# Gates' operands from GpSimd, the first pair's in u's weight buffers, and two groups of loads moved, in a decoder block

## The chip, the cores and the metric

One core of a Trainium2 chip runs the whole program. The metric is the device time of one execution in microseconds (us); the kernel before takes 2845.56 us (median of three runs, 2842.94 to 2846.51).

## What is computed

The reference is one decoder block on a sequence of 2048 tokens of width 1024. Cut to what matters here:

```python
h    = _rmsnorm(x, norm_pre_mix)
proj = h @ w_in                      # 1024 -> 5376 columns: q, k, v, u, z, gate_a, gate_b
u, z = gelu(proj[U0:Z0]), gelu(proj[Z0:GA0])
gate_a, gate_b = sigmoid(proj[GA0:GB0]), sigmoid(proj[GB0:])
y_attn = dilated_attention(q, k, v)  # 3 groups of 4 heads, merged by their log-denominators
y_gmlp = u * (spatial(layernorm(z)) + b_spatial)
merged = gate_a * (y_attn @ w_branch_attn) + gate_b * (y_gmlp @ w_branch_gmlp)
x = x + _rmsnorm(merged @ w_out)
a = relu(_rmsnorm(x) @ w_mlp_in)
x = x + _rmsnorm((a * a) @ w_mlp_out)
```

## The kernel before

Every product in float32 is made of three matmuls: each operand is split into a rounded part `hi` and a rest `lo`, and `mm3` (L91) adds hi·hi, hi·lo and lo·hi in PSUM. `split` (L68) makes both: `hi` by a copy on ACT, DVE or POOL, `lo` by a subtraction on DVE or POOL.

**Order of work.** TensorE's (PE's) instructions stay in the order in which the program is written; for ACT, DVE, POOL and the DMA queue of SP a scheduler of the framework fixes an order when the kernel is built. Each engine then works through its own list strictly in order, and an instruction that waits holds up all behind it. The stages up to the merge of the branches are:

1. q, k and v for all tokens (to L379), stored in DRAM.
2. `plain_1` (L468): u and z for the second half of the tokens. z is normalized, goes through the spatial product in `sz_out` (L419), is multiplied by u and stored as `ygd`. Weights come through `load_w` (L239) into the pool `wp`: tag `w` with six buffers, tag `raw` with two.
3. `seven` (L509): the gates of all tokens, and u of the first half, by Strassen's seven products. A pair is 256 columns of `w_in`; there are 16 pairs for the gates and two for u. For each pair `prepare` (L515) loads 1 MB of weights into `wr`, makes four sums of its quarters on POOL (L531 to L535), and splits seven operands (A11, S2, A12, S3, S1, A22, S4) into four places of `A_room`, `hi` on ACT, `lo` on DVE. A product is 12 matmuls of 512 columns (L560). Operand m+4 is prepared when product m is done, so a place is filled three products ahead of its use.
4. Attention: 48 units (`attn_unit`, L661), written between the steps of `seven` (a step is three matmuls) by the loop at L832. PE makes scores (`s`), DVE adds the mask and takes the maximum, one instruction of 128x4 on DVE (`nm`, L709) turns the maxima into the bias of ACT's exponentials, PE transposes (`pT`), ACT and DVE copy and split the result (`ph`, `pf`), PE multiplies by v (`pv`), ACT copies (`pvs`), PE transposes (`po`), and DVE reduces into `o` (L758). Scores, `pT`, `pv` and `po` share four PSUM buffers.
5. The combination (`combine`, L762): for each of four blocks of 512 tokens the three groups' results `A` are loaded, weighted on DVE (L769 to L786), added up (L788, L789: on DVE for the first block, else on POOL), transposed on PE (`yt`, L794) and stored. It too is written between steps of `seven`, the last 52.
6. `plain_0`: z for the first half, with the weights `z_w` loaded at L858; then the merge, for which `w_branch` is split into `wb` at L879.

After that come the output projection and the MLP, which the change does not touch.

**What lies around the change.** The first pair can only be prepared once z's weights have left `wp` (L816), since the pool `ap` with `wr` takes their room, and once the last of `H` has left tag `B12`, which `A_room` takes over (L512). The lines that set the steps around it are

```python
    steps(2 * 4 * 8 + 2 * 32 - 72 + 1)
    ew1.close()
    ap = stack(e1, "ap", 1)
    sm = stack(e1, "sm1", 2)
    steps(9)
    sz_out(*late.pop(0))
```

and attention's first loads follow `sz_out`, whose buffers they take.

Of the kernel before, what the change touches and what calls it, by code (L numbers as in the profile page):

```python
# [8 lines left out]
F32 = mybir.dt.float32  # L9
# [7 lines left out]
P = 128  # L17
# [24 lines left out]
def block_kernel(ctx, tc, a, out):  # L42
# [24 lines left out]
    def split(hi, lo, src, hi_eng="act", lo_eng="dve"):  # L67

        if hi_eng == "act":
            act.activation(hi, src, AF.Copy)  # L70
        elif hi_eng == "pool":
            pool.tensor_scalar(hi, src, 1.0, 1.0, op0=OP.mult, op1=OP.mult)  # L72
        else:
            dve.tensor_copy(hi, src)
        if behind_product is not None and lo_eng == "dve":
            behind_product.append((lo, src, f32(hi)))
        else:
            (pool if lo_eng == "pool" else dve).tensor_sub(lo, src, f32(hi))  # L78
# [82 lines left out]

    e1 = ExitStack()
    hp = stack(e1, "hp", 1)
    ew1 = ExitStack()
    wp = stack(ew1, "wp", 2)
    sm = stack(ew1, "sm", 2)
    st = stack(ew1, "st", 2)


    H = {}  # L170
# [60 lines left out]
    def w_src(i, kk):  # L231
        return a["w_in"][i, :, kk * 4:(kk + 1) * 4, :]

    n_w = 6

    def load_w(i, name):

        ws = []
        for kk in range(2):  # L239
            w = wp.tile([P, 2, 4, 256], F32R, name=f"{name}_{kk}", tag="w", bufs=n_w)  # L240
            raw = wp.tile([P, 4, 256], F32, name=f"{name}_r{kk}", tag="raw", bufs=2)
            split_in(w, w_src(i, kk), raw)
            ws.append(w)
        return ws
# [20 lines left out]
    def run(steps):  # L265
        for _ in steps:
            pass
# [197 lines left out]
    def plain_1():  # L465

        for q, (wi, kind, n, half) in enumerate(queue):
            if kind == "z" and n == 1:  # L468
                continue
            want(q)  # L470
            want(q + 1)
            if kind == "z" or (kind, n) == ("u", 1):
                want(q + 2)
            w = loaded[q]
            if kind == "z":
                for ci in range(2):
                    yield from z_chunk(zps[half], (w, loaded[q + 1]), half * 2 + ci)
                continue
            for ci in range(2):
                c = half * 2 + ci  # L480
                for m in range(2):
                    p = psum_mm(f"{kind}_{n}{m}{c}")
                    yield from steps_T(w, m, c, p)
                    t = st.tile([P, 512], F32, name=f"{kind}t_{n}{m}{c}", tag="ev", bufs=3)
                    act.activation(t, p, AF.Gelu_apprx_tanh)
                    sp.dma_start(u_d[n * 2 + m, :, c * 512:(c + 1) * 512], t)

# [8 lines left out]
    def load_op(half, name):  # L496

        pl = hp if name[0] == "B" else tp
        w = pl.tile([P, 2, 4, 512], F32R, name=f"{name}_b{half}", tag=name)
        if name[0] == "T":  # L500
            src = t1_d[half, :, int(name[1]) - 1]
        else:
            k = 4 * (int(name[1]) - 1)
            src = h_d[2 * half + int(name[2]) - 1, :, k:k + 4]
        for k in (0, 2):
            split_in(w[:, :, k:k + 2], src[:, k:k + 2], None, "act")
        ops[half, name] = w

    def seven():  # L509

        seq = [(p, *t) for p in pairs for t in SEVEN]
        room = hp.tile([P, 2, 4, 512], F32R, name="A_room", tag="B12")  # L512
        left, raws = {}, {}

        def prepare(m):  # L515
            if m >= len(seq):
                return
            pair, i, name, _ = seq[m]
            wi = pair[0]
            if name == "A11":  # L520
                raws["t"] = ap.tile([P, 2560], F32, name=f"wr_{m}", tag="wr")
                sp.dma_start(raws["t"][:, :2048], a["w_in"][wi].rearrange("p k c -> p (k c)"))
            t = raws["t"]
            q = t[:, :2048].rearrange("p (k c) -> p k c", c=256)
            a11, a12, a21, a22 = (q[:, k:k + 4, f:f + P] for f in (0, P) for k in (0, 4))
            s1 = t[:, 2048:].rearrange("p (k c) -> p k c", c=P)
            w = room[:, :, m % 4].rearrange("p o (k c) -> p o k c", k=4)
            split(w[:, 0], w[:, 1], dict(A11=a11, S2=a11, A12=a12, S4=a12, S3=a21, S1=s1, A22=a22)[name])
            left[m] = w
            if name == "A11":  # L530
                pool.tensor_add(s1, a21, a22)  # L531
                pool.tensor_sub(a21, a11, a21)
                pool.tensor_sub(a11, s1, a11)  # L533
            elif name == "A12":
                pool.tensor_sub(a12, a12, a11)  # L535

        def put(pair, f, ci, t):
            _, dst, n, half = pair
            if dst is u_d:
                act.activation(t, t, AF.Gelu_apprx_tanh)  # L540
            c = 2 * half + ci
            sp.dma_start(dst[2 * n + f, :, c * 512:(c + 1) * 512], t)

        for m in range(4):
            prepare(m)
        for m, (pair, i, name, bn) in enumerate(seq):
            half = pair[3]
            if i in (1, 6, 5):
                p = psum_mm(f"s{i}_{m}")
                if i == 1:  # L550
                    pa = p
                elif i == 6:
                    pb = p
                else:
                    pc = p
            p = {1: pa, 2: pa}.get(i) or ({6: pb, 7: pb, 4: pb}.get(i) or pc)
            w, h = left.pop(m), ops[half, bn]
            for k in range(4):
                for n, (l, r) in enumerate(((0, 0), (0, 1), (1, 0))):
                    pe.matmul(p, w[:, l, k, :], h[:, r, k, :], start=i in (1, 6, 5) and not k and not n,  # L560
                              stop=k == 3 and n == 2, skip_group_check=True)
                yield
            if i == 1:
                xs = ap.tile([P, 512], F32, name=f"xs_{m}", tag="xs", bufs=2)
                act.activation(xs, p, AF.Copy)
            elif i == 2:
                c1 = ap.tile([P, 512], F32, name=f"c1_{m}", tag="u", bufs=3)
                act.activation(c1, p, AF.Copy)
                put(pair, 0, 0, c1)
            elif i in (6, 7):  # L570
                u = ap.tile([P, 512], F32, name=f"u{i}_{m}", tag="u", bufs=3)
                dve.tensor_add(u, xs, p)
                if i == 6:
                    u6 = u
                else:
                    u7 = u
            elif i == 5:
                dve.tensor_add(u7, u7, p)
                put(pair, 1, 1, u7)
            elif i == 4:  # L580
                dve.tensor_add(xs, xs, p)
                put(pair, 1, 0, xs)
            else:
                dve.tensor_add(u6, u6, p)
                put(pair, 0, 1, u6)
            if half and pair[2] == 7:
                load_op(0, bn)
            prepare(m + 4)

    def plain_0():  # L590
# [9 lines left out]
    def filler():  # L600
        yield from plain_1()
        yield
        yield from seven()
        ended.append(True)
        yield
        yield from plain_0()

    fill = filler()

    def steps(n):  # L610
        for _ in range(n):
            next(fill, None)
# [199 lines left out]
    next(sg)  # L812
    steps(72)
    next(sg)
    steps(2 * 4 * 8 + 2 * 32 - 72 + 1)
    ew1.close()  # L816
    ap = stack(e1, "ap", 1)
    sm = stack(e1, "sm1", 2)
    steps(9)
    sz_out(*late.pop(0))  # L820
    ez.close()
    at1 = stack(e1b, "at1", 2, side="right")
    mask = at1.tile([P, 256], F32, name="mask", bufs=1)
# [1 line left out]
    attn_open(0, 0)  # L825
    attn_load(0, 0, 0)
    attn_load(0, 0, 1)
    steps(8)
    at = stack(e1b, "at", 2, side="right")
    steps(12)  # L830
    for n in range(len(units) + 1):
        u = None  # L832
        if n < len(units):
# [20 lines left out]
    e1b.close()  # L854
    n_w = 4
    wp = stack(e1, "wp2", 2)
    st = stack(e1, "st2", 1)
    z_w = [load_w(11 + n, f"w_z{n}0") for n in range(2)]  # L858
    ec = ExitStack()
    cb = stack(ec, "cb", 2, side="right")  # L860
    cs = [combine(c) for c in (2, 3, 0, 1)]
# [1 line left out]
        next(cs[n])  # L863
        next(cs[n])
    for n in range(4):
        steps((24, 14, 9, 5)[n])
        next(cs[n])
        if n < 2:
            next(cs[n + 2])
            next(cs[n + 2])  # L870
    ec.close()
    while not ended:
        steps(1)
    etp.close()
# [11 lines left out]
    steps(32)  # L886
    next(sg)
    run(fill)
    e1.close()


# [937 lines left out]
```

## Time and profile before

| | |
|---|---|
| median of three runs | 2845.56 us (2842.94 to 2846.51) |
| the profiled execution | 2839.19 us, of which the span of instructions 2837.5 us |
| PE matmuls | busy 2697.8 us, 95% of the span, 13196 instructions |
| DVE | busy 1695.6 us, 60% |
| ACT | busy 1131.5 us, 40% |
| POOL | busy 1054.2 us, 37% |
| granted clock of PE, mean | 0.978 of full speed |

PE is the engine with the most work. So one reads where PE stands idle or runs at the lower of its two clock levels (1.2 instead of 2.4 GHz, 0.5 in the profile), who ended each of its waits, and what stood ahead of that instruction in its engine's list. Busy time of the other engines matters only where it sits in such a chain. The stages above lie at 0 to 437.6 us (1), to 531.8 (2), to 574.4 (the start of 3 alone), to 1068.2 (3 and 4), to 1146.3 (5), and to the end (6 and the rest).

### The profile page before, as it was taken

To read this page: it belongs to the slowest core of one execution; us is meant where nothing else is said; L and a number is where in the kernel's file an instruction comes from. 1 tells how busy PE (TensorE), PEld (TensorE's weight loads), DVE (VectorE), ACT (ScalarE), POOL (GpSimd) and SP (SyncE) were. 2 spreads that over 40 slices of the span, in tenths; PEclk is the share of its full clock that TensorE was granted. 3 is DMA by queue.
4 is the path that set the end of the run, shared out by engine and by line. 5 is a ranking of instruction groups with operands and counts; after the bars stand their busy time and mean duration, and the time that the engine had idled before them with its cause. 6 is when DMAs were issued, how large, how long until landed. Compare 5 with 4: busy or idle time off the path is not lost. (4 is left out here: it accounts for less than half of the span.)

```text
span 2837.5 us, 36367 instructions
## 1 busy us (share of the span) xinstructions
PE 2697.8 (95%) x13196; PEld 2254.6 (79%) x13196; DVE 1695.6 (60%) x2839; ACT 1131.5 (40%) x2283; POOL 1054.2 (37%) x845
## 2 busy tenths in 40 slices
PE   8999999889989996899999899999999999999998
PEld 8889888778867885877778688888887877777787
DVE  5665563355566557565556654555445777777766
ACT  4213112145555443244344554555544222333334
POOL 2442541221111123311403532223323566776745
PEclk9999999999989998999999999999999999999999
DMA  8747654276575646465646734554334222222236
GB/s 282 231 141 226 213 151 146 92 234 185 178 259 181 179 156 225 124 227 158 197 146 219 234 115 123 159 192 131 100 118 135 66 82 82 85 86 82 82 98 214
DMA packets 327284, 449.17 MB, mean 158 GB/s; under 512 B 19008, under 2 KB 201536, under 8 KB 324800
## 3 DMA queue, kind: packets, MB, share of 16 engines
q1 hardware_dynamic: 239408, 395.71, 44.1%
q10 hardware_dynamic: 87696, 51.13, 6.0%
q8 instruction: 104, 1.70, 0.2%
q14 instruction: 76, 0.62, 0.1%
HBM read 295.58 MB, written 151.19 MB: 157 GB/s over the span
## 5 line engine op out<-in xcount | busy, mean ns | idle before, releaser
L1680 PE MATMUL ya<-T_spots,s 128*128 128x512 f32 x1272 | 313.3, 392 | 4.7 <-DVE acc L1688 2.7
L1680 PEld LDWEIGHTS ya<-T_spots,s 128*128 128x128 f32 x1272 | 239.0, 188 | 59.1 <-issue 4.5
L70 ACT ACTIVATE s<-sraw 128x768 fp32r<-128x768 f32 (+1 forms) x184 | 126.0, 695 | 358.5 <-POOL sraw L1479 199.4
L560 PE MATMUL s<-T_b,A_room 128*128 128x512 f32 x864 | 228.7, 406 | 1.3 <-DVE A_room L78 0.7
L1140 PE MATMUL aa<-B,A 128*128 128x512 f32 x768 | 186.6, 395 | 8.1 <-ACT xs L1154 5.8
L1111 POOL TENSOR_TENSOR s<-w1r 128x512 f32<-128x512 f32 x32 | 43.1, 1348 | 395.8 <-DVE S L78 330.3
L560 PEld LDWEIGHTS s<-T_b,A_room 128*128 128x128 f32 x864 | 160.4, 193 | 33.4 <-DVE A_room L78 1.4
L78 DVE TENSOR_TENSOR s<-sraw,s 128x512 fp32r<-128x512 f32 x171 | 163.7, 980 | 34.8 <-ACT s L70 33.2
L1140 PEld LDWEIGHTS aa<-B,A 128*128 128x128 f32 x768 | 145.1, 190 | 42.2 <-ACT xs L1154 6.2
L78 DVE TENSOR_TENSOR A_room<-wr,A_room 128x512 fp32r<-128x512 f32 x126 | 101.4, 808 | 117.8 <-ACT A_room L70 113.7
L1680 PE MATMUL yc<-T_spots,s 128*128 128x512 f32 x624 | 164.3, 394 | 3.6 <-POOL T_spots L78 3.6
L531 POOL TENSOR_TENSOR wr<-wr 128x512 f32<-128x512 f32 x18 | 24.4, 1353 | 360.6 <-DMA wr<-in_w_in_dram 352.3
L97 PE MATMUL x<-B,wq 128*128 128x512 f32 x384 | 150.7, 392 | 2.7 <-DVE wq L78 2.7
L95 PE MATMUL x<-B,wq 128*128 128x512 f32 x384 | 150.7, 393 | 0.7 <-POOL wq L72 0.7
L96 PE MATMUL x<-B,wq 128*128 128x512 f32 x384 | 150.4, 392 | 0.0
L1680 PEld LDWEIGHTS yc<-T_spots,s 128*128 128x128 f32 x624 | 115.9, 188 | 33.7 <-POOL T_spots L78 9.8
L78 POOL TENSOR_TENSOR T_spots<-w2r,T_spots 128x512 fp32r<-128x512 f32 x86 | 123.4, 1462 | 5.4 <-ACT T_spots L70 5.4
L70 ACT ACTIVATE A_room<-wr 128x512 fp32r<-128x512 f32 x126 | 78.0, 626 | 117.4 <-POOL wr L533 41.0
L70 ACT ACTIVATE hl<-r 128x512 fp32r<-128x512 f32 x48 | 30.4, 633 | 229.9 <-POOL r L291 86.0
L939 POOL TENSOR_TENSOR g<-g,g 128x512 f32<-128x512 f32 x28 | 38.8, 1386 | 189.8 <-DVE g L937 189.7
L1478 POOL TENSOR_TENSOR sraw<-sraw 128x256 f32<-128x256 f32 x56 | 41.5, 740 | 174.5 <-DVE s L78 160.2
L95 PE MATMUL o<-wo,mg 128*128 128x512 f32 x256 | 100.8, 394 | 4.3 <-ACT mg L70 4.3
(386 smaller groups left out, 7282.6 us busy)
## 6 DMA issues: line engine op xcount, KB each, us to landing
w1r<-in_w_mlp_in_dram SPq DMA_DIRECT2D x64, 512.0 KB, 3.8
sraw<-sd SPq DMA_DIRECT2D x128, 256.0 KB, 3.4
qk<-hl SPq DMA_DIRECT2D x24, 1024.0 KB, 5.3
qq<-qk SPq DMA_DIRECT2D x96, 256.0 KB, 4.7
wr<-in_w_in_dram SPq DMA_DIRECT2D x18, 1024.0 KB, 6.2
g<-gated SPq DMA_DIRECT2D x64, 256.0 KB, 4.1
w2r<-in_w_mlp_out_dram SPq DMA_DIRECT2D x16, 1024.0 KB, 6.4
sd<-u ACTq DMA_DIRECT2D x63, 256.0 KB, 2.9
```

Of the source, the lines that this page charges most:

```text
L70: act.activation(hi, src, AF.Copy)
L78: (pool if lo_eng == "pool" else dve).tensor_sub(lo, src, f32(hi))
L95: pe.matmul(ps, lh, rh, start=start, stop=False)
L96: pe.matmul(ps, lh, rl, start=False, stop=False)
L97: pe.matmul(ps, ll, rh, start=False, stop=stop)
L531: pool.tensor_add(s1, a21, a22)
L560: pe.matmul(p, w[:, l, k, :], h[:, r, k, :], start=i in (1, 6, 5) and not k and not n, stop=k == 3 and n == 2, skip_group_check=True)
L939: (dve if dt == KT - 1 else pool).tensor_add(parts[0], parts[0], parts[1])
L1111: pool.tensor_add(s1, a21, a22)
L1140: pe.matmul(p, w[:, l, k, :], h[:, r, k, :], start=i in (1, 6, 5) and not k and not n, stop=k == 3 and n == 2, skip_group_check=True)
L1478: pool.tensor_add(a22, a21, a22)
L1680: pe.matmul(p, s[:, l], w[:, r], start=i in (1, 2, 5) and not m and not o, stop=m == 1 and o == 2, skip_group_check=True)
```

## The change

- `prepare` splits the gates' operands on POOL alone, `hi` by a multiplication with 1 and `lo` by the subtraction. The two pairs of u keep `hi` on ACT, and `lo` is made by DVE and POOL in turn.
- The first pair is loaded in two halves into `raw` buffers of `wp`, and its first four operands go into two `w` buffers that u's weights had held. They are made during z (`next(sv)` after step 72). `A_room` is taken only for the fifth operand, and `wp` is closed inside `seven`, after the fourth product (`change`).
- Results of u and of the products share three buffers in a pool that stays open; `xs` has one buffer instead of two.
- 27 instead of 29 steps of `seven` stand between z and attention; `sz_out` comes after 8 instead of 9.
- z's weights for the first half are loaded inside the combination, after the second block's transposes are written, instead of ahead of it; and all that DVE and POOL get after the combination stays behind it in their lists (`issue_after`), `w_branch`'s splits among them. Steps of `seven` between the blocks: 24, 13, 9, 6 instead of 24, 14, 9, 5; the two that are left come after.

```diff
@@ seven @@
+            if m == 0:
+                src = [wp.tile([P, 4, 256], F32, name=f"wr_{kk}", tag="raw", bufs=2) for kk in range(2)]
+                for kk in range(2):
+                    sp.dma_start(src[kk], w_src(pair[0], kk))
+                raws["q"] = quarters(src)
+                raws["s1"] = st.tile([P, 512], F32, name="wr_s", tag="u", bufs=3).rearrange("p (k c) -> p k c", c=P)
+                for n in range(2):
+                    w = wp.tile([P, 2, 4, 256], F32R, name=f"A_first{n}", tag="w", bufs=n_w)
+                    rooms.update((2 * n + f, w[:, :, :, f * P:(f + 1) * P]) for f in range(2))
...
+            if m == 4:
+                room = hp.tile([P, 2, 4, 512], F32R, name="A_room", tag="B12")
+                rooms.update((n, room[:, :, n].rearrange("p o (k c) -> p o k c", k=4)) for n in range(4))
...
-            split(w[:, 0], w[:, 1], dict(A11=a11, S2=a11, A12=a12, S4=a12, S3=a21, S1=s1, A22=a22)[name])
+            if pair[1] is u_d:
+                split(w[:, 0], w[:, 1], src, "act", "dve" if m % 2 else "pool")
+            else:
+                split(w[:, 0], w[:, 1], src, "pool", "pool")
...
-                xs = ap.tile([P, 512], F32, name=f"xs_{m}", tag="xs", bufs=2)
+                xs = st.tile([P, 512], F32, name=f"xs_{m}", tag="xs")
...
+            if m == 3:
+                change()
@@ between z and attention @@
     steps(72)
     next(sg)
+    next(sv)
     steps(2 * 4 * 8 + 2 * 32 - 72 + 1)
-    ew1.close()
-    ap = stack(e1, "ap", 1)
-    sm = stack(e1, "sm1", 2)
+    steps(8)
+    sz_out(*late.pop(0))
     steps(9)
-    sz_out(*late.pop(0))
...
-    steps(8)
     at = stack(e1b, "at", 2, side="right")
-    steps(12)
+    steps(10)
@@ the combination @@
-    z_w = [load_w(11 + n, f"w_z{n}0") for n in range(2)]
...
-        steps((24, 14, 9, 5)[n])
+        steps((24, 13, 9, 6)[n])
...
+        if n == 1:
+            z_w = [load_w(11 + m, f"w_z{m}0") for m in range(2)]
     ec.close()
+
+    es = ExitStack()
+    for e in (mybir.EngineType.DVE, mybir.EngineType.Pool):
+        es.enter_context(tc.issue_after(next(i for i in reversed(nc.cur_bb.bb.instructions) if i.engine == e)))
```

**Where instructions go.** SP's list at the end of z, before (`ur` and `ygd` belong to `sz_out`, `wr` is the first pair's weights):

```order
L436 DMA ygd<-sb_4580 128x512
L436 DMA ygd<-sb_4591 128x512
L429 DMA ur_4603<-ud 128x512
L429 DMA ur_4614<-ud 128x512
L436 DMA ygd<-sb_4602 128x512
L429 DMA ur_4757<-ud 128x512
L436 DMA ygd<-sb_4613 128x512
L522 DMA wr_4700<-in_w_in_dram 128x2048
L429 DMA ur_4768<-ud 128x512
L436 DMA ygd<-sb_4756 128x512
```

and with the change (`ud` is u's store, ahead of z's end):

```order
L486 DMA ud<-ut_4049 128x512
L536 DMA wr_4241<-in_w_in_dram 128x1024
L536 DMA wr_4242<-in_w_in_dram 128x1024
L486 DMA ud<-ut_4097 128x512
L429 DMA ur_4600<-ud 128x512
L429 DMA ur_4611<-ud 128x512
L486 DMA ud<-ut_4125 128x512
L486 DMA ud<-ut_4153 128x512
L486 DMA ud<-ut_4181 128x512
L436 DMA ygd<-sb_4599 128x512
```

The first pair's load stood behind all four stores of `sz_out`'s first block; now its two halves go out among u's stores, while z is being computed.

POOL's list for one pair of gates during attention, before (after the last multiplication of `sz_out`):

```order
L435 TENSOR_TENSOR sb_4789<-sb_4789,ur_4790 128x512
L531 TENSOR_TENSOR wr_4842<-wr_4842 128x512
L532 TENSOR_TENSOR wr_4842<-wr_4842 128x4x128
L533 TENSOR_TENSOR wr_4842<-wr_4842 128x4x128
L535 TENSOR_TENSOR wr_4842<-wr_4842 128x4x128
```

and with the change, the first 12 rows of one pair (6 rows of splits follow):

```order
L72 TENSOR_SCALAR A_room<-wr_5043 128x512
L561 TENSOR_TENSOR wr_5043<-wr_5043 128x512
L78 TENSOR_TENSOR A_room<-wr_5043,A_room 128x512
L562 TENSOR_TENSOR wr_5043<-wr_5043 128x4x128
L563 TENSOR_TENSOR wr_5043<-wr_5043 128x4x128
L72 TENSOR_SCALAR A_room<-wr_5043 128x512
L78 TENSOR_TENSOR A_room<-wr_5043,A_room 128x512
L72 TENSOR_SCALAR A_room<-wr_5043 128x512
L78 TENSOR_TENSOR A_room<-wr_5043,A_room 128x512
L565 TENSOR_TENSOR wr_5043<-wr_5043 128x4x128
L72 TENSOR_SCALAR A_room<-wr_5043 128x512
L78 TENSOR_TENSOR A_room<-wr_5043,A_room 128x512
```

Four sums become four sums and fourteen halves of operands; the operand S2 is whole with the seventh row.

DVE's list in the combination, before, ahead of the first block's weights (`M`, `E`, `A` are the combination's, `w_z` z's weights, `u`, `xs` the products'):

```order
L78 TENSOR_TENSOR w_z_0_9453<-w_z_r_9454,w_z_0_9453 128x1024
L78 TENSOR_TENSOR w_z_1_9458<-w_z_r_9459,w_z_1_9458 128x1024
L578 TENSOR_TENSOR u_115_9599<-u_115_9599,s_116_9608 128x512
L769 TENSOR_TENSOR M_9480<-A_9476 128x16
L581 TENSOR_TENSOR xs_9548<-xs_9548,s_113_9552 128x512
L78 TENSOR_TENSOR w_z_0_9463<-w_z_r_9464,w_z_0_9463 128x1024
L584 TENSOR_TENSOR u_113_9565<-u_113_9565,s_116_9608 128x512
L78 TENSOR_TENSOR w_z_1_9468<-w_z_r_9469,w_z_1_9468 128x1024
L770 TENSOR_TENSOR M_9480<-M_9480,A_9476 128x16
L773 TENSOR_TENSOR E_9483<-A_9476,M_9480 128x4x4 x3
```

and with the change, from the end of the first block to the second block's twelve multiplications:

```order
L78 TENSOR_TENSOR A_room<-wr_9582,A_room 128x512
L807 TENSOR_TENSOR E_9494<-A_9487,M_9491 128x4x4 x3
L78 TENSOR_TENSOR A_room<-wr_9582,A_room 128x512
L78 TENSOR_TENSOR w_z_0_9789<-w_z_r_9790,w_z_0_9789 128x1024
L811 TENSOR_TENSOR Z_9499<-E_9494,A_9487 128x4x4 x3
L812 TENSOR_TENSOR M_9491<-Z_9499 128x16
L78 TENSOR_TENSOR w_z_1_9794<-w_z_r_9795,w_z_1_9794 128x1024
L813 TENSOR_TENSOR M_9491<-M_9491,Z_9499 128x16
L615 TENSOR_TENSOR u_113_9546<-u_113_9546,s_116_9589 128x512
L814 RECIPROCAL M_9491<-M_9491 128x16
L816 TENSOR_TENSOR E_9494<-E_9494,M_9491 128x4x4 x3
L820 TENSOR_TENSOR A_9487<-A_9487,E_9494 128x256 x12
```

The `lo` of z's weights no longer stands ahead of the first block; it stands inside the second block (two of the four) and inside the third and fourth (one each), where each waits for its `hi` on POOL.

## Rows read from the trace of the kernel before

**Rows 1.** Windows view: stretch, length, busy PE, PEld, DVE, ACT, POOL, clock, DMA, GB/s.

```profile
531.80:579.00 47.20, 31.98 (x135) 25.27 (x136) 23.58 (x41) 12.13 (x22) 18.71 (x14) 0.78 0.62 190
579.00:1068.20 489.20, 455.62 (x2476) 388.55 (x2475) 283.13 (x760) 247.26 (x691) 82.98 (x61) 0.97 0.62 192
784.00:858.00 74.00, 59.58 (x292) 49.27 (x291) 49.82 (x107) 42.92 (x102) 10.67 (x8) 0.86 0.75 245
1068.20:1146.30 78.10, 44.95 (x190) 35.64 (x189) 63.91 (x136) 24.72 (x40) 37.76 (x20) 0.84 0.71 231
```

**Rows 2.** Waits of PE, 531.8 to 579 us.

```profile
PE s L560 <- ACT A_room L70: 9.8, 2, 9.2
PE s L688 <- DMA qq<-qk: 4.8, 1, 4.8
```

**Rows 3.** Timeline, 531.5 to 575 us, PE and then SP.

```profile
550.45 3.73 PE L425 MATMUL sz<-wsp,z 128*128 128x128 f32 x32
...
556.11 8.40 PE L560 MATMUL s<-T_b,A_room 128*128 128x512 f32 x36
...
574.41 0.55 PE L688 MATMUL s<-kp,qq 128*128 128x256 f32 x1 [4.76 <-DMA qq<-qk]
...
560.38 0.32 SPq L436 DMA_DIRECT2D ygd<-sb  x1
562.51 0.32 SPq L542 DMA_DIRECT2D gated<-u  x1
```

**Rows 4.** Waits of PE, 579 to 1068.2 us.

```profile
PE pT L732 <- DVE o L758: 12.0, 5, 4.4
```

**Rows 5.** Timeline, 627 to 631 us, DVE and then PE.

```profile
628.42 0.69 DVE L78 TENSOR_TENSOR A_room<-wr,A_room 128x512 fp32r<-128x512 f32 x1 [2.60 <-ACT A_room L70]
629.03 0.68 DVE L758 TENSOR_REDUCE o<-po 128x256 f32<-128x512 f32 x1
...
629.77 0.66 PE L732 MATMUL pT<-ident,e 128*128 128x128 f32 x4 [1.94 <-DVE o L758]
```

**Rows 6.** Lines view of DVE, 579 to 1068.2 us: busy us, mean ns | idle before.

```profile
L78 DVE TENSOR_TENSOR A_room<-wr,A_room 128x512 fp32r<-128x512 f32 x105 | 82.3, 787 | 101.7 <-ACT A_room L70 100.4 <-PE s L560 0.6
```

**Rows 7.** Lines view of POOL by form, whole span: busy us, mean ns | idle before.

```profile
L78 POOL TENSOR_TENSOR yt<-yt 128x512 fp32r<-128x512 f32 x6 | 8.0, 1348 | 0.2
...
L72 POOL TENSOR_SCALAR yt<-yt 128x512 fp32r<-128x512 f32 x6 | 4.0, 675 | 18.3 <-DMA yt<-yad 18.3
```

**Rows 8.** Timeline, POOL at 623 us and PE at 640 us: one pair.

```profile
623.39 1.29 POOL L531 TENSOR_TENSOR wr<-wr 128x512 f32<-128x512 f32 x1 [21.35 <-DMA wr<-in_w_in_dram]
...
640.61 2.24 PE L560 MATMUL s<-T_b,A_room 128*128 128x512 f32 x9
```

**Rows 9.** Timeline, DVE and POOL at 805 us, DVE at 822 us.

```profile
805.90 1.23 DVE L709 TENSOR_SCALAR nm<-o 128x4 f32<-128x4 f32 x1
...
805.66 1.44 POOL L531 TENSOR_TENSOR wr<-wr 128x512 f32<-128x512 f32 x1 [34.30 <-DMA wr<-in_w_in_dram]
...
822.08 0.15 DVE L709 TENSOR_SCALAR nm<-o 128x4 f32<-128x4 f32 x1
```

**Rows 10.** Waits of PE, 1068.2 to 1146.4 us.

```profile
PE yt L794 <- POOL A L789: 19.4, 3, 14.8
PE yt L794 <- issue: 12.5, 1, 12.5
```

**Rows 11.** Timeline of the combination: SP, DVE, POOL.

```profile
1072.58 0.93 SPq L766 DMA_DIRECT2D A<-att  x2
...
1080.14 2.48 SPq L766 DMA_DIRECT2D A<-att  x4
...
1085.42 1.22 DVE L78 TENSOR_TENSOR w_z<-w_z_r,w_z 128x1024 fp32r<-128x1024 f32 x1
...
1089.61 4.11 DVE L786 TENSOR_TENSOR A<-A,E 128x256 f32<-128x256 f32 x12
...
1137.70 3.30 POOL L788 TENSOR_TENSOR A<-A 128x1024 f32<-128x1024 f32 x1
```

More of the change, by code (lines that the diff above doesn't have):

```diff
@@ L163, in block_kernel @@
     hp = stack(e1, "hp", 1)
+    st = stack(e1, "st", 1)
     ew1 = ExitStack()
@@ L166, in block_kernel @@
     sm = stack(ew1, "sm", 2)
-    st = stack(ew1, "st", 2)
     H = {}
@@ L483, in plain_1 @@
                     yield from steps_T(w, m, c, p)
-                    t = st.tile([P, 512], F32, name=f"{kind}t_{n}{m}{c}", tag="ev", bufs=3)
+                    t = st.tile([P, 512], F32, name=f"{kind}t_{n}{m}{c}", tag="u", bufs=3)
                     act.activation(t, p, AF.Gelu_apprx_tanh)
@@ L507, in load_op, with change, quarters @@
         ops[half, name] = w
+    def change():
+        nonlocal ap, sm
+        ew1.close()
+        ap = stack(e1, "ap", 1)
+        sm = stack(e1, "sm1", 2)
+    ap = None
     def seven():
         seq = [(p, *t) for p in pairs for t in SEVEN]
-        room = hp.tile([P, 2, 4, 512], F32R, name="A_room", tag="B12")
-        left, raws = {}, {}
+        left, raws, rooms = {}, {}, {}
+        def quarters(t):
+            return [t[k // 4][:, :, f:f + P] for f in (0, P) for k in (0, 4)]
         def prepare(m):
@@ L518, in prepare @@
             pair, i, name, _ = seq[m]
[L519 to L527, printed above, removed]
-            split(w[:, 0], w[:, 1], dict(A11=a11, S2=a11, A12=a12, S4=a12, S3=a21, S1=s1, A22=a22)[name])
+            if m == 0:
[7 more added lines that the diff above has]
+                    rooms.update((2 * n + f, w[:, :, :, f * P:(f + 1) * P]) for f in range(2))
+            elif name == "A11":
+                t = ap.tile([P, 2560], F32, name=f"wr_{m}", tag="wr")
+                sp.dma_start(t[:, :2048], a["w_in"][pair[0]].rearrange("p k c -> p (k c)"))
+                t8 = t[:, :2048].rearrange("p (k c) -> p k c", c=256)
+                raws["q"] = quarters((t8[:, :4], t8[:, 4:]))
+                raws["s1"] = t[:, 2048:].rearrange("p (k c) -> p k c", c=P)
+            if m == 4:
+                room = hp.tile([P, 2, 4, 512], F32R, name="A_room", tag="B12")
+                rooms.update((n, room[:, :, n].rearrange("p o (k c) -> p o k c", k=4)) for n in range(4))
+            a11, a12, a21, a22 = raws["q"]
+            s1 = raws["s1"]
+            w = rooms[m % 4]
+            src = dict(A11=a11, S2=a11, A12=a12, S4=a12, S3=a21, S1=s1, A22=a22)[name]
+            if pair[1] is u_d:
+                split(w[:, 0], w[:, 1], src, "act", "dve" if m % 2 else "pool")
+            else:
+                split(w[:, 0], w[:, 1], src, "pool", "pool")
             left[m] = w
@@ L545, in seven @@
             prepare(m)
+        yield
         for m, (pair, i, name, bn) in enumerate(seq):
@@ L563, in seven @@
             if i == 1:
-                xs = ap.tile([P, 512], F32, name=f"xs_{m}", tag="xs", bufs=2)
+                xs = st.tile([P, 512], F32, name=f"xs_{m}", tag="xs")
                 act.activation(xs, p, AF.Copy)
             elif i == 2:
-                c1 = ap.tile([P, 512], F32, name=f"c1_{m}", tag="u", bufs=3)
+                c1 = st.tile([P, 512], F32, name=f"c1_{m}", tag="u", bufs=3)
                 act.activation(c1, p, AF.Copy)
@@ L570, in seven @@
             elif i in (6, 7):
-                u = ap.tile([P, 512], F32, name=f"u{i}_{m}", tag="u", bufs=3)
+                u = st.tile([P, 512], F32, name=f"u{i}_{m}", tag="u", bufs=3)
                 dve.tensor_add(u, xs, p)
@@ L602, in filler @@
         yield
-        yield from seven()
+        yield from sv
         ended.append(True)
@@ L606, in filler @@
         yield from plain_0()
+    sv = seven()
     fill = filler()
@@ L856, in block_kernel @@
     wp = stack(e1, "wp2", 2)
-    st = stack(e1, "st2", 1)
-    z_w = [load_w(11 + n, f"w_z{n}0") for n in range(2)]
     ec = ExitStack()
@@ L888, in block_kernel @@
     run(fill)
+    es.close()
     e1.close()
```

## The prediction

> **What bounds the kernel now.** PE has the most work, and the end of the program comes as late as PE is kept idle. I read its busy time by stretches first, then its waits in three of them, then the lists of the engines that ended those waits. From the start of `seven` to the end of the combination PE stands still for 15.2, 33.6 and 33.1 us (length less busy PE) [rows 1]; its granted clock there is 0.78, 0.97 and 0.84, so a part of the matmuls also runs at 1.2 instead of 2.4 GHz. These three stretches are all that the change touches, and what can be won is about 82 us of waiting and some of the time at the lower clock.
>
> The first stretch waits 9.8 us for operands of the first pair, then 4.8 us for attention's first load [rows 2]. Attention waits in pieces of 1 to 4 us, most of all (12.0 us) for `o` [rows 4]. One piece shows the pattern: DVE's list has the `lo` of a gate's operand ahead of the reduction into `o`; that `lo` began only at 628.42, since its `hi` came late from ACT, so `o` ended at 629.71, and the transposes that need its PSUM buffer stood 1.94 us [rows 5]. In that stretch DVE makes 105 such `lo` of 0.787 us and stood 101.7 us before them, nearly all of it for ACT [rows 6]. The combination waits 31.9 us for its weighted sums [rows 10].
>
> **The sum, made against the profiled execution (2839.19 us).** The median of the runs stands 6.4 us above that execution; what I take off the one I take off the other.
>
> *Start of seven: 12 us less.* Stretch one begins where z's last matmul ends, 531.8. Before, attention's first scores start at 574.41 [rows 3]. With the change the first four operands are ready, so PE goes on at once. A step costs 0.70 us (36 matmuls, 12 steps, in 8.40) and the spatial product 3.73 [rows 3]: 27 steps and that product are 22.6 us, PE is there at 554.4. But it will then wait for attention's first load, whose buffers come free by `sz_out`'s stores. From the start of the spatial product to its fourth store it took 9.9 us (550.45 to 560.38), from there to the scores 14.0, of which SP stood 1.8 us before `gated<-u` [rows 3], which the change puts behind these loads. The spatial product now starts after eight steps, at 537.4. I add 0.6 us, as POOL splits three operands ahead of `sz_out`'s multiplications, and get 537.4 + 9.9 + 0.6 + 12.2 = 560.1. That is 14.3 us sooner; two steps (1.4 us) are only moved to the end, and about 1 us I give to the second pair, whose sums and splits start late. Bounds: 18.6 less if the load is no longer late, 6 less if POOL's new work holds the multiplications for all its six instructions (3 x (0.675 + 1.348) = 6.1 us [rows 7]).
>
> *Attention: 19 us less.* ACT loses the `hi`, DVE the `lo` of 105 operands, which are what stood ahead of the late instructions. The waits of 784 to 858 us, 14.4 us [rows 1], have a second cause: there the operands for the first half of the tokens are loaded and split, still on ACT and DVE. I let a third of these go (4.4), and three quarters of the other 19.2 us (14). The clock was at half for about 3% x 2 of 489 us, 29 us, more than half of it idle; I take 4 us back. Against that, 3 us for what POOL now does to DVE (below). Bounds: all 33.6 us and 7 of clock, 40 less; no gain at all, or the loss that `nm` brings (below).
>
> Can POOL carry it? For one pair it has four sums of about 1.3 us and seven times 0.675 + 1.348 [rows 7, 8], 19.4 us, against some 30 us that a pair takes in attention (455.6 us of PE's work for 15 pairs, or 105 operands [rows 1, 6]). POOL has 83 us of work there now [rows 1]. The tightest operand is S2: after the load lands POOL needs `hi`, sum, `lo`, two sums, `hi`, `lo`, 7.9 us. In the pair at 623 us the load had landed when the sum began, and the product with S2 began 17.2 us later [rows 8]. So there the cover is 9 us; if the cover goes, PE waits by what is missing, once a pair.
>
> *What POOL does to DVE.* `nm` (128x4) takes 0.15 us alone, but 1.23 us when POOL's sum runs: it ended at 807.13, the sum at 807.10 [rows 9]. So this small instruction stands until POOL's is done. The Trainium skill ("SBUF — State Buffer", Who interferes with whom) says that DVE's second port pair is POOL's too and is held for a whole instruction, so that one fully blocks the other when DVE runs in a two-port mode or reads two tensors from SBUF; this trace agrees with 1.23 against 0.15. By that rule each `nm` that meets POOL's work is late by up to 1.1 us; by the rows it has met it seldom, since POOL was idle for five sixths of the time. With POOL busy for some 60% of it, 48 units have a delay of 0.3 to 0.5 us on average. I price it at 3 us, for between the scores and `pv` PE has five or six steps of `seven` (3.5 to 4.2 us), and DVE's reductions, maxima and splits from PSUM are not held up. Bounds: 0 and 48 x 1.08 = 52.
>
> *Combination: 3 us less.* The first block's third load was issued at 1080.14, behind z's weights [rows 11]; now all six loads stand together, and it goes at about 1073.5. So the first wait (12.5 us [rows 10]) shrinks to 6 or 7. Then comes what the move costs. z's weights need four `lo` on DVE, 1.22 us each alone [rows 11], now between the second and fourth block's steps; two of them wait for `hi` that POOL makes only after the second block's sums, some 6 us (3.3 us for one of two at worst [rows 11]). The twelve multiplications (4.1 us [rows 11]) stand behind that. So I put the second wait at 10, the third at 7; the fourth, 14.8 us [rows 10] with four of `w_branch`'s splits ahead, falls to 6 with two ahead. That is 30 in place of 31.9, a little clock more, less the two steps that come after. Bounds: 15 less (DVE keeps ahead), 10 more (the stand behind POOL comes in all three blocks).
>
> Later stages keep their order on all engines; `w_branch` is split during z, ahead of the merge. 12 + 19 + 3 = 34 us: 2805 for the profiled execution, **2812 us** for the median.
>
> **Rivals.**
> - *Attention stays as it is* (18%): the waits for ACT and DVE have other causes (the exponentials ahead of `pf`, the loads at 784 us), and `nm`'s delay takes the rest. For it: the 14.4 us. Against: rows 5. Only start and combination remain: 2845.6 - 15 = 2831 us.
> - *The combination gains too* (12%): with z's weights out of the way of the first block the later ones do not pile up, 15 instead of 3: 2800 us.
> - *Slower* (7%): PE is held for `nm` in every unit. Place: the split `ph` behind `nm` on DVE, and `pv` behind that. Price: 52 us at most, against 15 us at start and combination and 22 in attention. It decides when DVE reaches `ph` less than about 1 us before PE needs it; in rows 5's unit, `o` late by 2 us, PE still had a margin. All of it: 2845.6 - 37 + 52 = 2861 us.
> - *Nothing to measure* (4%): half of that. Within 0.2% (5.7 us), which is what a measurement of this kernel can tell from no change.
>
> **How the numbers follow.** The forecast has 59%; its own terms run from about 2796 to 2826. The range reaches to the combination's 2800 and to the 2831 of unchanged attention: 2792 to 2834. Out of it stay the slower case (7%), no change (4%) and the ends of the others (8%). Faster by over 0.2% are the forecast, the combination's rival and nearly all of the first rival: 88%; within 0.2%: 5%; slower: 7%.
>
> **What would show it.** No wait of PE for the first pair's operands, attention's scores 14 us after the earlier place, and a wait of about 5 us for their load. In attention PE's idle time at 12 to 20 us instead of 33.6, and POOL busy for 300 us or more; `nm` at 0.4 to 0.7 us on average. In the combination four waits of similar length, about 30 us in sum. I am wrong if PE waits for operands that POOL makes, if `ph` behind `nm` becomes the longest wait of attention, or if the combination's waits differ from 30 us by more than 12.

## The result, and the profile after

The changed kernel takes 2799.24 us (median of four runs, 2795.09 to 2799.81) against 2845.38 us: a ratio of 0.9836 (changed to before), 95% interval 0.9819 to 0.9853, or 46 us less (42 to 51). The forecast was 34 us less, 2812 us. The sign and the range hold; the gain is a third larger than the sum of the terms.

The windows view of the changed kernel, with the columns of [rows 1] and the same three parts (the rest of the start with the first units, attention, the combination):

```profile
532.90:568.10 35.20, 28.68 (x126) 23.62 (x126) 15.29 (x29) 3.38 (x5) 22.19 (x22) 0.86 0.66 206
568.10:1031.20 463.10, 449.29 (x2478) 387.01 (x2478) 220.88 (x659) 194.58 (x593) 277.59 (x267) 0.98 0.66 205
1031.20:1109.10 77.90, 49.85 (x199) 40.02 (x198) 61.27 (x128) 28.64 (x41) 37.48 (x23) 0.82 0.61 200
```

PE's idle time (length less busy PE) fell from 15.2 to 6.5 us at the start, from 33.6 to 13.8 in attention and from 33.1 to 28.1 in the combination. In attention POOL has 277.6 us of work instead of 83.0, DVE 220.9 instead of 283.1, ACT 194.6 instead of 247.3. The combination, in contrast, is as long as before (77.9 us; 78.1 in [rows 1]).

Waits of PE in attention and then in the combination (total, times, longest, in us), to be held against [rows 4] and [rows 10]. Where a row says `issue`, the profile names nothing that PE waited for:

```profile
PE s L591 <- DVE u L603: 5.7, 2, 3.8
PE pv L785 <- DVE ph L772: 4.6, 3, 2.3
PE s L722 <- DMA qq<-qk: 4.0, 1, 4.0
PE s L591 <- POOL A_room L78: 1.5, 1, 1.5
PE pv L785 <- ACT pf L779: 1.5, 1, 1.5
...
PE yt L828 <- POOL A L823: 19.3, 3, 7.4
PE yt L828 <- issue: 6.7, 1, 6.7
PE s L591 <- ACT xs L596: 2.1, 1, 2.1
```

Three more rows of before in attention:

```profile
PE pv L751 <- ACT pf L745: 6.8, 5, 2.1
PE po L757 <- ACT pvs L753: 6.6, 5, 2.5
PE pv L751 <- DVE ph L738: 6.0, 4, 3.4
```

The wait for `o` (12.0 us) is gone, and those for `pvs` with it; those for `pf` and `ph` are shorter. Of the 106 `lo` that POOL makes in attention one was late, by 1.5 us, at 977.7 us. Apart from it and the load, what is left lies between 760 and 806 us, where the operands for the first half of the tokens are split on ACT and DVE.

Parts of the program in all the traces below, in us: from z's last matmul to attention's first scores; to the last `po`; to the first matmul of z for the first half; and from the first matmul of the merge to the end, whose instructions are the same in all of them. Runs are medians; a ratio is to the kernel before, run beside each group of kernels (its medians are 2842.4 to 2845.4 us).

| kernel | runs | ratio (95%) | start | attention | combination | merge to end |
|---|---|---|---|---|---|---|
| before | 2845.4 | 1 | 42.6 | 493.8 | 77.7 | 1643.6 |
| changed | 2799.2 | 0.9836 (0.9819 to 0.9853) | 30.6 | 467.7 | 77.5 | 1637.7 |
| e1 POOL's part alone | 2807.1 | 0.9865 (0.9844 to 0.9886) | 43.4 | 460.0 | 78.9 | 1643.4 |
| e5 start alone | 2831.5 | 0.9965 (0.9952 to 0.9978) | 30.9 | 492.6 | 83.9 | 1643.2 |
| e2 all but POOL's part | 2823.5 | 0.9922 (0.9904 to 0.9941) | 31.7 | 495.4 | 78.2 | 1643.0 |
| e3 all but the combination | 2808.7 | 0.9874 (0.9852 to 0.9895) | 31.5 | 465.7 | 83.8 | 1648.8 |
| e6 hi ACT, lo POOL | 2840.0 | 0.9989 (0.9978 to 1.0001) | 31.5 | 505.4 | 78.2 | 1642.5 |
| e7 hi POOL, lo DVE | 2829.6 | 0.9957 (0.9943 to 0.9970) | 30.2 | 491.3 | 78.2 | 1645.9 |
| e8 29 steps | 2800.6 | 0.9851 (0.9836 to 0.9867) | 30.6 | 466.2 | 77.1 | 1645.4 |
| e4 `nm` on ACT | 2790.6 | 0.9810 (0.9790 to 0.9831) | 31.8 | 454.6 | 78.2 | 1643.1 |
| e9 before, `nm` on ACT | 2833.7 | 0.9965 (0.9951 to 0.9979) | 43.6 | 493.8 | 79.4 | 1643.0 |
| e12 the same again | 2837.4 | 0.9978 (0.9962 to 0.9994) | 42.7 | 490.7 | 78.6 | 1644.1 |
| e10 e4, sums on DVE | 2789.4 | 0.9802 (0.9780 to 0.9824) | 30.6 | 455.6 | 70.7 | 1643.0 |
| e11 e10, half of lo on POOL | 2790.3 | 0.9811 (0.9786 to 0.9836) | 31.4 | 461.6 | 72.8 | 1644.9 |

The last column is a warning: the same work took 1637.7 to 1648.8 us, and the shortest is the changed kernel's own profile. The 5.9 us that it seems to gain there over the kernel before are no effect of the change: the other seven kernels with all of the change's later code (e2, e4, e6, e7, e8, e10, e11) stand at 1642.5 to 1645.9, and the profiled execution of the changed kernel, 2795.09 us, is the fastest of its four by 4 us.

### The profile page after: what moved, and what is told of

The parts are those of the page before. It is cut to its first block, busy times and chain, and to the rows that moved or that the text cites. A ratio compares the mean times of both kernels' runs of the same rounds, so it can differ in the third digit from the quotient of the medians.

```text
span 2793.3 us, 36446 instructions
## 1 busy us (share of the span) xinstructions
PE 2687.1 (96%) x13196; PEld 2251.0 (81%) x13196; DVE 1627.1 (58%) x2720; ACT 1076.3 (39%) x2175; POOL 1267.4 (45%) x1076
## 5 line engine op out<-in xcount | busy, mean ns | idle before, releaser
L591 PE MATMUL s<-T_b,A_room 128*128 128x512 f32 x840 | 221.6, 406 | 7.2 <-DVE u L603 5.7
L78 POOL TENSOR_TENSOR A_room<-wr,A_room 128x512 fp32r<-128x512 f32 x114 | 149.2, 1309 | 15.6 <-ACT A_room L70 8.5
L72 POOL TENSOR_SCALAR A_room<-wr 128x512 fp32r<-128x512 f32 x107 | 69.3, 648 | 175.8 <-DMA wr<-in_w_in_dram 99.8
L792 DVE TENSOR_REDUCE o<-po 128x256 f32<-128x512 f32 x48 | 33.1, 691 | 126.0 <-PE po L791 126.0
```

## Experiments: the three parts, one at a time

**e1**, POOL's part alone, in the kernel before:

```diff
-            split(w[:, 0], w[:, 1], dict(A11=a11, ...)[name])
+            engs = ("pool", "pool") if m > 6 and pair[1] is not u_d else ("act", "dve")
+            split(w[:, 0], w[:, 1], dict(A11=a11, ...)[name], *engs)
```

> The kernel before, with one part of the change: from the second pair on, the gates' operands are split by POOL alone; start, loads and combination stay. Theory (the attention term: ACT's hi and DVE's lo stood ahead of late instructions): attention is shorter by about the 26 us that the whole change took there, so 2817 to 2826 us. Rival (attention gained because it starts in another state, its operands earlier by the new start): attention as long as before, 2842 to 2847 us. The stretch after the merge's start should stay at 1643 us by both; if it falls by 6 us here too, that part varies by itself.

Measured: 2807.06 us, 38 us less than before (32 to 44), more than the theory's 28 at most. The start is as before, attention 33.8 us shorter; its windows row:

```profile
575.40:1035.40 460.00, 448.88 (x2490) 386.50 (x2491) 225.01 (x669) 196.39 (x594) 276.49 (x269) 0.99 0.68 208
```

PE is idle for 11.1 us and its clock is 0.99. So attention's gain stands by itself; nothing of the new start is needed for it.

**e2**, the changed kernel without POOL's part:

```diff
-                split(w[:, 0], w[:, 1], src, "pool", "pool")
+                split(w[:, 0], w[:, 1], src, *(("pool", "pool") if m < 7 else ("act", "dve")))
```

> The changed kernel with that part undone: from the second pair on, hi on ACT and lo on DVE again; the new start and the new combination stay. Theory: attention back near 494 us, so 2818 to 2828 us in all, and the start keeps its 11 to 12 us. Rival (the start or the loads brought attention's gain): under 2806 us.

Measured: 2823.47 us, as the theory had it. Attention is back at 495.4 us, the start keeps its 31.7. Its waits in attention:

```profile
PE po L791 <- ACT pvs L787: 6.1, 6, 2.5
PE pv L785 <- ACT pf L779: 5.0, 6, 1.5
PE s L591 <- DVE u L603: 4.7, 2, 2.8
PE s L722 <- DMA qq<-qk: 4.6, 1, 4.6
PE pT L766 <- DVE o L792: 4.3, 2, 2.5
PE s L591 <- DVE u L609: 3.9, 4, 1.4
```

In these rows ACT is late for 11.1 us and DVE for 12.9, and nothing of attention's gain came from the start or the loads.

**e3**, the changed kernel with the combination as before:

```diff
+    z_w = [load_w(11 + n, f"w_z{n}0") for n in range(2)]
     ec = ExitStack()
...
-        steps((24, 13, 9, 6)[n])
+        steps((24, 14, 9, 5)[n])
...
-        if n == 1:
-            z_w = [load_w(11 + m, f"w_z{m}0") for m in range(2)]
...
-    for e in (mybir.EngineType.DVE, mybir.EngineType.Pool):
+    for e in ():
```

> The changed kernel with the combination as before: z's weights loaded ahead of it, nothing of DVE and POOL held behind it, steps 24, 14, 9, 5. Theory (the combination term is 2 to 3 us, the 6 us after the merge's start have nothing to do with it): 2799 to 2804 us, the combination's waits again one long, two short, one long. Rival (what is held behind the combination also gives the 6 us of the merge and the 1 us of z): 2805 to 2811 us. Third possibility: the move costs, and this is faster than the changed kernel, under 2797 us.

Measured: 2808.73 us, outside the theory's 2799 to 2804 and in the rival's range. The pattern of one long, two short and one long wait came back as the theory said:

```profile
PE yt L828 <- POOL A L823: 19.0, 3, 13.2
PE yt L828 <- issue: 13.5, 1, 13.5
```

But the rival's reason doesn't hold: the combination itself is longer by 6.3 us than in the changed kernel, and of the merge's 1648.8 us nothing can be put down to the old order, since e5, which has that order too, stands at 1643.2. The old order takes not the 77.7 us of before here, but 83.8:

```profile
1028.30:1112.40 84.10, 51.12 (x197) 40.96 (x196) 62.27 (x131) 25.79 (x39) 40.67 (x24) 0.76 0.60 200
```

This is not more waiting. PE is idle for 33.0 us, as in [rows 1] (33.1), and busy for 6.2 us more. Two more steps are 1.4 us of that; the rest is the lower clock, 0.76 against 0.84 in [rows 1] and 0.82 in the changed kernel.

**e5**, only the new start (the edits of e2 and e3 together):

> The changed kernel with both other parts undone: from the second pair on hi on ACT and lo on DVE, the combination as before. Only the new start is left. Theory (the three parts add up): attention's first scores 11 to 12 us sooner, attention and combination as before but for two steps that come later, 2831 to 2835 us. Rival (the new start shifts the products against the attention's units and costs or gives something there): attention differs from 494 us by 5 us or more, and the time by as much.

Measured: 2831.52 us, within the theory's range. The start is 11.7 us shorter, attention 492.6 us. And the combination in the old order again takes 83.9 us: with 27 steps ahead of attention instead of 29, two more are left for it (1.4 us by [rows 3]), and it loses some 5 us more (here 2.1 of the 6.2 us are waiting, PE's idle time being 35.2 us). That the products stand differently against its blocks would explain it; no run takes the steps apart from the rest of the new start. So the move of z's weights is worth about 6 us by the profiles of e3 and e5 against those of the changed kernel and e2; seen from before it only repays what the new start costs there.

In the order start, combination, attention the ratios give 0.9965, 0.9922 and 0.9836: 10 us (6 to 14), 12 and 24 us, the last two uncertain by 6 or 7. Taken first, POOL's part gave 38. These 38 and 24 differ by 14 us, more than the 9 or so of their uncertainty; why stays open. In the profiles attention gains 33.8 us in e1 and 27.7 from e2 to the changed kernel.

## Experiments: which half of an operand matters

**e6**: `hi` on ACT, `lo` on POOL. **e7**: `hi` on POOL, `lo` on DVE. Both in the changed kernel, from the second pair on:

```diff
-                split(w[:, 0], w[:, 1], src, "pool", "pool")
+                split(w[:, 0], w[:, 1], src, *(("pool", "pool") if m < 7 else ("act", "pool")))    # e6
+                split(w[:, 0], w[:, 1], src, *(("pool", "pool") if m < 7 else ("pool", "dve")))    # e7
```

> The changed kernel, but from the second pair on hi is made by ACT and lo by POOL: DVE is relieved, ACT is not. Theory (both lists held late work; of the waits with ACT and DVE doing the splits, about half name ACT and half DVE): between the two, 2806 to 2814 us. Rival 1 (DVE's lo, standing before a late hi, is the whole cause): 2796 to 2802 us, as the changed kernel. Rival 2 (ACT's hi is): 2818 us or more.

> The mirror image: from the second pair on hi by POOL, lo by DVE: ACT is relieved, DVE is not, and its lo now stands before POOL's hi. Theory: between the two as well, 2806 to 2816 us. If DVE's lo is the whole cause, 2818 us or more; if ACT's hi is, 2796 to 2802 us.

Measured: 2839.98 and 2829.64 us. The theory fell twice. Each kernel came out where the half that it leaves in its place was to be the whole cause, which can't hold for both: moving one half alone brings nothing. Against e2, which has both halves on ACT and DVE (0.9922), e6 is 0.67% slower (0.9989) and e7 0.35% (0.9957). The waits of PE in attention, of e6:

```profile
PE pv L785 <- ACT ph L771: 13.0, 6, 3.0
PE po L791 <- ACT pvs L787: 12.1, 8, 3.7
PE pv L785 <- ACT pf L779: 5.6, 7, 2.1
```

and of e7:

```profile
PE s L591 <- DVE u L609: 10.6, 4, 3.4
PE pT L766 <- DVE o L792: 7.8, 2, 4.6
PE s L591 <- DVE u L603: 5.2, 2, 2.8
```

The engine that keeps a half is the engine that is late. The worst wait of e6 shows how, in rows of ACT, POOL and PE from the timelines:

```profile
974.79 0.63 ACT L70 ACTIVATE A_room<-wr 128x512 fp32r<-128x512 f32 x1 [3.13 <-POOL wr L563]
975.33 0.58 ACT L787 ACTIVATE pvs<-pv 128x512 f32<-128x512 f32 x1
...
972.15 1.27 POOL L78 TENSOR_TENSOR A_room<-wr,A_room 128x512 fp32r<-128x512 f32 x1
973.50 1.26 POOL L563 TENSOR_TENSOR wr<-wr 128x512 f32<-128x512 f32 x1
...
975.96 1.12 PE L791 MATMUL po<-ident,pvs 128*128 128x128 f32 x4 [3.75 <-ACT pvs L787]
```

ACT's next in line is the `hi` of S2, whose source is POOL's sum. POOL makes a `lo` first, then the sum. ACT stands idle for 3.13 us, `pvs` behind it, and PE 3.75 us. In e7 it is DVE that stands, before POOL's `hi`, with `o` behind it:

```profile
588.62 1.20 POOL L72 TENSOR_SCALAR A_room<-wr 128x512 fp32r<-128x512 f32 x2
...
589.27 1.08 DVE L78 TENSOR_TENSOR A_room<-wr,A_room 128x512 fp32r<-128x512 f32 x1 [3.20 <-POOL A_room L72]
590.27 0.68 DVE L792 TENSOR_REDUCE o<-po 128x256 f32<-128x512 f32 x1
...
591.01 0.90 PE L766 MATMUL pT<-ident,e 128*128 128x128 f32 x3 [4.61 <-DVE o L792]
```

So it isn't the work that ACT and DVE are rid of: e6 takes as much from DVE as the change does (222.9 us busy in attention, 220.9 in the changed kernel). It is the wait for what the other engine makes of the operand, its sum in e6 and its `hi` in e7, at the head of an in-order list with attention's urgent work behind it. That wait doesn't go with one half: ACT stood 157.0 us before its `hi` in attention of e6 and 131.9 in e2, DVE 89.5 us before its `lo` in e7 and 84.6 in e2. With both halves and the sums on POOL that wait is on an engine on which attention has nothing.

## Experiments: what attention still loses, and nm

**e8**: `steps(10)` to `steps(12)` ahead of attention.

> The changed kernel with 29 steps of the products ahead of attention, as before, instead of 27: two more matmul steps lie under the wait for attention's first load, and the products stand against the attention's units as they did before. Theory (after POOL has the operands, what attention still loses at 763 and 776 us comes from where the products' sums on DVE fall in a unit): the wait for the load falls from 4 to about 2.6 us, attention to about 460 us as in the kernel with POOL's part alone, 2788 to 2793 us. Rival (the place within the unit doesn't matter, only the two steps under the wait count): 1.4 us less, attention 466 to 468 us, 2796 to 2800 us.

Measured: 2800.56 us, no difference from the changed kernel (0.9851 against 0.9836). The wait for the load fell from 4.5 to 1.8 us, but ahead of it PE waited 1.4 us for an operand of the second pair from POOL. The waits at 763 and 776 us made room for others (`pf` 5.7, `ph` 3.1, `o` 2.6 us, in the same places as in e1, counted from attention's start, and `pvs` 2.3). Attention is 466.2 us. The theory fell: in these two kernels the place within the unit decides which instruction is late, not how much in sum (13.7 and 13.8 us). Why attention is 6 us shorter still in e1 stays open.

**e4**, in the changed kernel, and **e9**, in the kernel before:

```diff
-        dve.tensor_scalar(nm_t, ot[:, :, 260 + j], -0.125, None, op0=OP.mult)
+        act.activation(nm_t, ot[:, :, 260 + j], AF.Copy, scale=-0.125)
```

> The changed kernel with nm made by ACT instead of DVE, so that POOL's work can't hold it. Theory (the hold costs about 3 us, PE has other work in between): 2794 to 2799 us, attention's waits of PE nearly the same. Rival (the hold sits in many units behind the remaining waits): attention 8 us shorter or more, under 2791 us.

> The kernel before with nm on ACT alone: there POOL is idle for five sixths of attention, so hardly an nm is held. Theory (what the changed kernel gained by nm on ACT came from POOL's hold on DVE): 0 to 3 us less than before, 2840 to 2845 us. Rival (the gain is the shorter way from the maxima to the exponentials, without a change of engine, whatever POOL does): 8 us less or more, under 2837 us.

Measured: e4 2790.61 us, at the rival's bound, with attention 13 us shorter in its profile. The hold is there, as the mean of `nm` in attention shows, of the changed kernel and then of before:

```profile
L743 DVE TENSOR_SCALAR nm<-o 128x4 f32<-128x4 f32 x48 | 21.4, 446 | 0.7
```

```profile
L709 DVE TENSOR_SCALAR nm<-o 128x4 f32<-128x4 f32 x47 | 11.0, 234 | 1.0
```

But e9 is also 0.35% faster than before (0.21 to 0.49), without any new work on POOL, as its rival said; its profile doesn't show where (attention 493.8 us).

**e12**, the same kernel as e9:

> The kernel before with nm on ACT a second time, for a second profile: by its runs it was 0.35% under before, but its profiled execution was the slowest of twelve and showed attention no shorter than before (493.8 us). If the shorter way from the maxima to the exponentials gains in attention without any new work on POOL, attention is 484 us or less here, and the waits that end with ACT or with ph are fewer. If attention stays within 3 us of 493.8 again, the gain of its runs lies elsewhere and stays open.

Measured: 0.22% faster (0.06 to 0.38), attention 490.7 us, 3.1 less than before: far from the 484 that would have placed the gain in attention, and just outside the 3 us that would have placed it elsewhere. So `nm` on ACT gives some 6 to 10 us by the runs, with POOL's new work and without it. That the shorter way from the maxima to the exponentials is the reason is argued and not shown, as no profile shows where the gain of e9's runs lies. What is left in e4 for POOL's hold can't be told from nothing: my 3 us are neither shown nor excluded.

## Experiments: towards a faster version

**e10**: e4, with `eng = dve` for the combination's sums in all four blocks.

> The changed kernel with nm on ACT, and the combination's sums on DVE for all four blocks. Of nm alone 2791 us are known. Theory (each of the last three waits of the combination ends with two sums on POOL, 2.4 and 3.3 us, and POOL's sums hold the small DVE instructions of the next block, 2.0 to 2.3 us instead of 0.2): those three waits fall by about 3 us each, the combination from 78 to about 70 us, 2781 to 2785 us. Rival (DVE, busy for most of the combination, becomes its bound): the waits stay and end with DVE, 2788 us or more.

Measured: the combination falls to 70.7 us. Its waits for the sums are 6.7, 3.2, 5.8 and 2.6 us, against 6.7, 6.9, 5.0 and 7.4 in the changed kernel. The last three of the changed kernel and then of e10:

```profile
1076.53 1.97 PE L828 MATMUL yt<-ident,A 128*128 128x128 f32 x8 [6.89 <-POOL A L823]
1090.79 1.90 PE L828 MATMUL yt<-ident,A 128*128 128x128 f32 x8 [5.04 <-POOL A L823]
1105.02 1.33 PE L828 MATMUL yt<-ident,A 128*128 128x128 f32 x5 [7.37 <-POOL A L823]
```

```profile
1063.53 1.74 PE L828 MATMUL yt<-ident,A 128*128 128x128 f32 x8 [3.16 <-issue]
1078.21 1.94 PE L828 MATMUL yt<-ident,A 128*128 128x128 f32 x8 [5.80 <-issue]
1088.88 1.07 PE L828 MATMUL yt<-ident,A 128*128 128x128 f32 x8 [2.64 <-issue]
```

Two of the last three waits fell by about 4 us, one rose a little. The runs (2789.41 us) can't tell it from e4's 2790.61, though the profile shows 7.5 us less in this part (the profiled execution, 2782.81 us, is the fastest of five). Expected were 2781 to 2785; the time lies where the rival had it, 2788 or more, but the waits did not stay as it had them. e4, e10 and e11 below are the fastest kernels of the study, 7 to 10 us under the changed one by their ratios; the ends of their intervals still overlap with its own.

**e11**: e10, with the `lo` of the second half of each operand that is loaded in attention on POOL:

```diff
-            split_in(w[:, :, k:k + 2], src[:, k:k + 2], None, "act")
+            split_in(w[:, :, k:k + 2], src[:, k:k + 2], None, "act", "pool" if half == 0 and k else "dve")
```

> As the one before, and of the operands for the first half of the tokens that are split in the middle of attention, the second half of each gets its lo from POOL instead of DVE. Theory (the waits left there are DVE's backlog from these lo of 1.2 to 1.6 us): 3 to 5 us less than the kernel before it. Rival (hi on ACT and lo on POOL puts a wait at the head of POOL's list, as with the gates' operands, and holds up the gates' own): the same or slower by up to 8 us.

Measured: 2790.27 us, no gain. Attention is 6 us longer in the profile, and PE's waits at 794, 824 and 827 us (1.8, 1.6 and 1.7 us) now end with POOL's `A_room`: the rival's picture, as e6's with the engines changed.

## Why the prediction was right, and what was mis-sized

- **Start, 12 us less**: the scores come 12.0 us sooner after z's end, where 14.3 were worked out; less the two steps that only move (1.4), that is 10.6, and the runs of e5 give 10 (6 to 14). PE had no wait for the first pair's operands, and 4.5 us for the load (forecast: about 5). The chain to the scores (563.52, with z's end 1.1 us later than before) is 2.3 us longer than worked out. The spatial product began 1.1 us late, as PE waited 1.2 us for `z` on DVE, its fourth store came 12.5 us after its beginning instead of 10.5, and the load took 0.8 less. Behind the first of these stands POOL's hold on DVE, which the forecast set only against `nm`. Two of the small steps of z's normalization on DVE took 1.25 and 1.20 us and ended within 0.03 us of two of POOL's new splits; before they took 0.17 and 0.16. DVE and POOL of the changed kernel, then DVE of before:

```profile
536.13 1.25 DVE L112 TENSOR_SCALAR t_ln<-t_ln 128x4 f32<-128x4 f32 x1
537.41 1.20 DVE L113 TENSOR_TENSOR r_ln<-r_ln,t_ln 128x4 f32<-128x4 f32 x1
...
536.06 1.29 POOL L78 TENSOR_TENSOR A_room<-wr_s,A_room 128x512 fp32r<-128x512 f32 x1
537.31 1.27 POOL L78 TENSOR_TENSOR A_room<-wr,A_room 128x512 fp32r<-128x512 f32 x1
```

```profile
534.68 0.17 DVE L112 TENSOR_SCALAR t_ln<-t_ln 128x4 f32<-128x4 f32 x1
534.88 0.16 DVE L113 TENSOR_TENSOR r_ln<-r_ln,t_ln 128x4 f32<-128x4 f32 x1
```

- **Attention, 19 us less**: 26.1 in the profile, 24 by e2 against the changed kernel and 38 by e1. This term was too small. Its waits fell from 33.4 us without the load's to 13.8, 19.6 where I had 18.4 (by the shares that I named, a third of 14.4 and three quarters of 19.2, it would have been 19.2). The rest is busy PE, 455.6 to 449.3 us, 6.3 where I had taken 4 for the clock, and the 3 us set against it for `nm`, of which the waits show nothing: all waits for DVE's `ph` are three, 4.6 us, all between 790 and 804 us, where DVE splits `T_b` and `B_b`. The reading of [rows 5] was right, and e6 and e7 make it sharper: what counted was the wait before the `lo`, not its 0.787 us [rows 6].
- **POOL as the carrier**: 277.6 us of work there, some 18 less than the 83 + 105 x 2.02 of the forecast's rows; its halves take 649 and 1305 ns in attention, about as in [rows 7]. By the letter the forecast's sign "PE waits for operands that POOL makes" came true, once, for 1.5 us.
- **Combination, 3 us less**: the waits are 6.7, 6.9, 5.0 and 7.4 us, 26 in sum (forecast: 6 to 7, 10, 7, 6, together 30), with 2.1 for `xs` on ACT as a new one. Its length is that of before, as the clock fell from 0.84 to 0.82 and two more steps lie in it. Mis-sized was the base: I held the new order against the old combination of before, but with the new start the old one takes 84 us (e3, e5). Against that the move is worth 6 us by the profiles, and 12 (6 to 18) by the runs of e5 and e2.
- **The rest, 0**: the profile has 1.0 us less in z, where the other traces differ by 1.9, and 5.9 less from the merge on. There this one execution stands below all others (1642.5 to 1648.8 us, with the new code 1642.5 to 1645.9), so the 5.9 us are no gain of the change.
- **Where the 12 us between 34 and 46 lie**: by the runs the start gave 2 less than forecast, attention 5 more and the combination 9 more, each uncertain by 4 to 7.
- **Rivals**: attention unchanged fell with e1 and e2. The slower case fell as no `ph` was late for `nm` outside the loads' stretch. The measured 2799 us is the 2800 of the rival in which the combination gains 15, but that rival isn't shown: by the runs the combination gives 12, by the profiles 6 against e3 and nothing against before, and attention gave more than forecast as well.
- **A word of the forecast**: its "attention's scores 14 us after the earlier place" means 14 us ahead of it, as its sum has it.

## What to carry to other kernels

Where an operand is made in two dependent halves, let one engine make both, one on which nothing urgent is queued: here a half left on the busy engine left the wait there, and cost more than the work saved. (No run puts both halves on one busy engine, so which of the two conditions counts more isn't shown.) Before counting how much work an engine is rid of, look at what stands first in its list and what it waits for. And where one edit shifts the start of later stages, hold a later edit against the shifted program, not against the one that was profiled.

## What the hardware showed

POOL's hold on DVE is larger in the combination than at `nm`. DVE's maximum `M` of 128x16 takes 0.17 us where POOL is idle (the two of L804 ahead of 1060 us); so does the addition `M<-Z` of the same shape, in the last row. Beside POOL's sums of 128x1024 in the changed kernel it took 1.98 and 2.31 us, ending with them (1087.41 and 1087.37, 1090.77 and 1090.74):

```profile
1085.43 1.98 DVE L803 TENSOR_TENSOR M<-A 128x16 f32<-128x16 f32 x1 [0.27 <-DMA A<-att]
1087.33 1.21 DVE L78 TENSOR_TENSOR w_z<-w_z_r,w_z 128x1024 fp32r<-128x1024 f32 x1
1088.46 2.31 DVE L804 TENSOR_TENSOR M<-M,A 128x16 f32<-128x16 f32 x1
...
1094.41 0.17 DVE L812 TENSOR_TENSOR M<-Z 128x16 f32<-128x16 f32 x1
```

```profile
1084.91 2.46 POOL L822 TENSOR_TENSOR A<-A 128x1024 f32<-128x1024 f32 x1 [6.25 <-DVE A L820]
1087.45 3.29 POOL L823 TENSOR_TENSOR A<-A 128x1024 f32<-128x1024 f32 x1
```

It goes both ways: POOL's second sum has a DVE subtraction of 1.21 us beside it and takes 3.29 us instead of 2.46. The Trainium skill ("SBUF — State Buffer", Who interferes with whom) calls the contention for the ports that the two share an exclusive lock, under which the one that comes second fully blocks and is not just slowed; this trace agrees, with 2.31 us against 0.17. DVE's splits `ph`, which take one of their two inputs from PSUM, are not held: they take 551 ns on average in attention of the changed kernel and 554 in e2, where POOL has a third of the work. The splits of `T_b`, with both inputs in SBUF, are: 1631 ns on average against 1352.
